# Recurrence of a hybrid decoder layer: sums of split tiles, key products in four array quarters, and the samples' chunk stacked on 128 partitions

## The chip, the cores and the metric

The kernel runs on one core of a Trainium2 chip. The metric is the device time of one execution in microseconds; of the kernel before, three runs were timed. The engines are named as in the profile: PE is TensorE (PEld its weight loads), DVE VectorE, ACT ScalarE, POOL GpSimd, SP SyncE, which issues most of the DMAs.

## What is computed

The reference is one step of a decoder layer with two branches, a recurrence and a sparse attention, between two feed-forward blocks. The change lies in the recurrence, for 512 tokens of one prompt and 4 new tokens of each of 8 sample sequences, with 8 heads of width 64. Cut to what matters:

```python
def rwkv7_time_mix(p, prev, s0, mu, w0, w2, a0, a2, g2, k_k, k_a, r_k, ln_w, ln_b):
    xs = p + (p_prev - p) * mu
    r, k, v, wd, ad, gd = jnp.split(xs, ...)
    log_w = -softplus(-(w0 + tanh(wd) @ w2)) - 0.5
    decay = exp(-exp(log_w))
    a = sigmoid(a0 + ad @ a2)                      # rate
    g = sigmoid(gd) @ g2                           # gate
    kk = heads(k * k_k)
    kk = kk * rsqrt(maximum(sum(kk * kk, -1), 1e-24))      # key norms
    k = k * (1 + (a - 1) * k_a)
    def step(S, inp):
        sa = einsum('bhij,bhj->bhi', S, -kk_t)
        S = S * w_t[:, :, None, :] + sa[..., None] * (kk_t * a_t)[:, :, None, :] + v_t[..., None] * k_t[:, :, None, :]
        return S, einsum('bhij,bhj->bhi', S, r_t)
    s_final, y = lax.scan(step, s0, (r_h, w_h, k_h, v_h, kk, a_h))
    y = group_norm(y) * ln_w + ln_b
    bonus = sum(r_h * k_h * r_k, -1) * v_h
    return (y + bonus) * g, p[:, -1], s_final
```

## The kernel before

Activations lie with features on the partitions and the 544 tokens (512 of the prompt, 32 of the samples) in the columns; matmuls over all tokens run in two halves of 272. Dense layers use split tiles: a tile is kept as a rounded half `hi` and a rest `lo`, both of type f32r, and a product is the sum of two or three f32r matmuls. The recurrence before the change uses plain f32 tiles throughout, except for the final output `yah`.

The recurrence handles the 8 heads in four pairs. I call a pair a head, as the code does (`rw_head`, `ht` = 0 to 3). Each head is a Python generator that goes through these pieces:

- `rw_front` (L1605): loads; decay rates; rate product with `a2t`; key norms, which are sums over 64 partitions by a matmul with the 0/1 matrix `blk` (`head_sums`, L1598, matmul L1602); decay sums, which are running sums over the 64 tokens of a chunk by matmuls with the 0/1 matrix `tri` (L1650); then elementwise work that gives the key tiles `ar`, `be`, `ka`.
- `rw_prompt` (L1689): the prompt in 8 chunks of 64 tokens. `products` (L1703, matmul L1710) multiplies keys by keys. A triangular system is then inverted in blocks of 16, 32 and 64: the blocks of 16 in fifteen small steps, whose row selections are matmuls (L1738: `sel` as the stationary tile, `dd` moving) and whose two small DVE operations a step are L173 and L179. Then come the inverse of 32 (from L1770 on), u1 and u2 (L1815), the chunk matrices (L1830), and seven steps from chunk to chunk (L1863).
- `rw_sample` (L1890): the same for the 8 short sequences as one chunk of 32 columns, with the matmuls of `by_head` (L1900), each with a `tile_position` in the array. After it the state is written out, and the bonus sums (a `head_sums` with a copy `brk` of `blk`, scaled by r_k) and the gate product with `g2t` (also L1602) follow.
- `rw_tail` (L1991): group norm and gate, output to `yah` (cast L2010, subtraction L179).

Four heads may be under way (`RW_LIVE`), and a head starts nine turns after the one ahead of it (`RW_LAG`); each turn of the loop advances every live head by one `yield`. That only sets program order and with it priorities. A scheduler of the tile framework sets each engine's queue from dependencies, free buffers and priorities, so that a small edit can move instructions of several heads against each other. Between the small products it also places a dense filler, `wob_steps` (L2031, matmul L288 in `dense_half`), at a lower priority. Tiles come from pools with a fixed number of buffers: a tile that has no free buffer waits until the readers of an older one are done. PSUM has two double-bank tiles `mm` and four single-bank tiles `sm`.

```python
        said = next(g_, heads)
        if said is heads:
            live.remove(g_)
        elif said is True:
            with tc.high_priority(offset=-WOB_OFF):
                next(wst, None)
```

## Time and profile before

| | |
|---|---|
| median of three runs | 1766.99 us (1765.64 to 1770.39) |
| profiled execution | 1762.41 us |
| its span | 1760.6 us |
| mean granted clock of TensorE in it | 0.979 of full speed |
| busy in the span | PE 1673.3 us (95%), DVE 876.6 (50%), ACT 612.8 (35%), POOL 245.9 (14%) |

The profile is one execution, recorded by the hardware. Busy time is the time in which an engine had an instruction running; matmuls overlap and their ends are modelled, so a busy PE need not be PE at its peak. PEclk is the share of full clock that TensorE was granted in a stretch (1.00 is 2.4 GHz, 0.50 is 1.2 GHz). The chain of work goes back from the last instruction: at each step to what released it, or to the instruction before it on its engine; its rows have a start, a length and a count of like instructions. Idle time stands with the engine and line that ended it. The recurrence lies between about 1000 and 1246 us of the span.

### The profile page before, as it was taken

The page shows a single profiled execution, that of the slowest core. Times are in us where ns is not written, and L with a number is a line of the kernel's source. Part 1 is how long each engine was busy: PE and PEld are TensorE (multiplying, and loading weights), DVE is VectorE, ACT ScalarE, POOL GpSimd, SP SyncE. Part 2 cuts the span into 40 slices and gives each one's busy share as a digit, 9 for nine tenths or more (in the row PEclk, how much of TensorE's full clock was granted, in tenths as well). Part 3 has the DMA queues.
Part 4 walks back from the last instruction along what each step waited for, and adds up shares of the span by engine and source line. Part 5 has one row for each costly group of instructions (what it writes and reads, how often), then busy time and mean ns, then how long its engine had stood idle before and what let it go on. Part 6 is the DMA issues. An engine that isn't in the chain of part 4 may idle for free.

```text
span 1760.6 us, 34894 instructions
## 1 busy us (share of the span) xinstructions
PE 1673.3 (95%) x14727; PEld 1518.0 (86%) x14727; DVE 876.6 (50%) x1835; ACT 612.8 (35%) x1121; POOL 245.9 (14%) x304
## 2 busy tenths in 40 slices
PE   5999999999999899899898999999899999999997
PEld 4888899999988798677786977777898999999996
DVE  6664323323325835555558376766767333333345
ACT  4343221221223543343445352332456321222223
POOL 6640000000000312535300011221011000000000
PEclk9999999999999999999999997999999999999998
DMA  7863553563434185565422331211651433223221
GB/s 269 307 198 114 179 192 109 173 204 118 146 110 101 49 280 170 156 211 164 141 74 85 117 94 45 72 28 35 208 139 45 125 87 94 85 83 98 83 74 52
DMA packets 261348, 225.01 MB, mean 128 GB/s; under 512 B 28948, under 2 KB 225983, under 8 KB 260936
## 3 DMA queue, kind: packets, MB, share of 16 engines
q1 hardware_dynamic: 244928, 180.39, 34.1%
q0 software_dynamic: 10368, 35.79, 6.2%
q10 hardware_dynamic: 5896, 6.60, 1.1%
q8 instruction: 116, 1.90, 0.4%
q14 instruction: 40, 0.33, 0.1%
HBM read 199.57 MB, written 23.17 MB: 127 GB/s over the span
## 4 chain that ended last, share of the span: by engine, by line
PE 78%; DVE 7%; issue 5%; ACT 3%; DMA 3%; POOL 3%; SPq 0%; POOLq 0%; ACTq 0%; DVEq 0%
PE mm L279 46%; PE mm L288 7%; PE mm L400 5%; PE sm L519 2%; PE sm L288 2%; POOL sraw L1300 1%; PE sm L1900 1%; PE mm L1602 1%; PE mm L2107 1%; PE sm L1246 1%; PE sm L1738 1%; DMA raw<-in_phi_w1t_dram 1%; DMA raw<-in_w_o_dram 1%; PE sm L1710 1%; PE mm L1208 1%
## 5 line engine op out<-in xcount | busy, mean ns | idle before, releaser
L261 ACT CAST whi<-raw 128x1024 fp32r<-128x1024 f32 (+2 forms) x178 | 177.3, 997 | 655.7 <-PE mm L279 594.8
L279 PE MATMUL mm<-uh,whi 128*128 128x272 f32 (+1 forms) x1888 | 397.5, 292 | 3.6 <-ACT qs L193 1.3
L279 PE MATMUL mm<-uh,wlo 128*128 128x272 f32 (+1 forms) x1888 | 392.9, 289 | 1.0 <-DVE wlo L179 1.0
L279 PE MATMUL mm<-ul,whi 128*128 128x272 f32 (+1 forms) x1888 | 392.3, 289 | 0.0
L179 DVE TENSOR_TENSOR wlo<-raw,whi 128x1024 fp32r<-128x1024 f32 (+2 forms) x178 | 206.1, 1158 | 263.0 <-ACT whi L261 261.6
L279 PEld LDWEIGHTS mm<-uh,whi 128*128 128x128 f32 x1888 | 298.4, 189 | 23.3 <-ACT hh L880 9.2
L279 PEld LDWEIGHTS mm<-ul,whi 128*128 128x128 f32 x1888 | 299.9, 189 | 1.0 <-issue 1.0
L279 PEld LDWEIGHTS mm<-uh,wlo 128*128 128x128 f32 x1888 | 297.6, 189 | 2.5 <-DVE wlo L179 1.4
L173 DVE TENSOR_TENSOR sg<-mm,sg 128x544 f32<-128x544 f32 (+1 forms) x47 | 32.3, 687 | 161.6 <-PE mm L279 159.1
L400 PE MATMUL mm<-cx,w1h 128*128 128x256 f32 x512 | 100.4, 291 | 3.7 <-ACT cx L352 1.9
L676 POOL TENSOR_TENSOR xT<-xT,mr 128x272 f32<-128x272 f32 x24 | 25.4, 1076 | 532.1 <-DVE xT L173 519.9
L279 PE MATMUL mm<-hh,wlo 128*128 128x256 f32 x480 | 99.5, 289 | 0.0
L279 PE MATMUL mm<-hh,whi 128*128 128x256 f32 x480 | 99.4, 288 | 0.0
L279 PE MATMUL mm<-hlo,whi 128*128 128x256 f32 x480 | 99.3, 288 | 0.0
L400 PEld LDWEIGHTS mm<-cx,w1h 128*128 128x128 f32 x512 | 82.6, 193 | 11.2 <-issue 6.7
L279 PEld LDWEIGHTS mm<-hh,whi 128*128 128x128 f32 x480 | 77.2, 188 | 1.7 <-ACT hh L880 1.7
L279 PEld LDWEIGHTS mm<-hh,wlo 128*128 128x128 f32 x480 | 77.2, 188 | 0.0
L279 PEld LDWEIGHTS mm<-hlo,whi 128*128 128x128 f32 x480 | 77.2, 188 | 0.0
L400 PE MATMUL mm<-cx,w1l 128*128 128x256 f32 x256 | 73.8, 288 | 0.0
L1300 POOL DMA_INDIRECT sraw<-in_cache_kv_sel_dram,idx x64 | 64.0, 1001 | 58.1 <-PE sm L1313 37.0
L821 DVE TENSOR_TENSOR rtmp<-mm,modT 128x32 f32<-128x32 f32 x32 | 6.1, 191 | 117.9 <-PE mm L279 117.9
L182 DVE SCALAR_TENSOR_TENSOR xT<-mm,modT,xT 128x512 f32<-128x512 f32 (+2 forms) x80 | 46.4, 582 | 35.5 <-PE mm L288 35.2
(566 smaller groups left out, 2978.3 us busy)
## 6 DMA issues: line engine op xcount, KB each, us to landing
araw<-in_w_ada_dram SPq DMA_DIRECT2D x56, 512.0 KB
raw<-in_ffn_w_gate_dram SPq DMA_DIRECT2D x44, 512.0 KB
raw<-in_ffn_w_up_dram SPq DMA_DIRECT2D x44, 512.0 KB
raw<-in_w_in_dram SPq DMA_DIRECT2D x36, 512.0 KB
raw<-in_ffn_w_down_dram SPq DMA_DIRECT2D x32, 448.0 KB
raw<-in_w_ada_dram SPq DMA_DIRECT2D x16, 512.0 KB
raw<-in_ffn_w_down_dram SPq DMA_DIRECT2D x16, 512.0 KB
sraw<-in_state_kv_win_dram SPq DMA_DIRECT2D x16, 256.0 KB
```

Source lines behind the costliest of these rows:

```text
L173: V.tensor_tensor(out, a, b, ALU.mult)
L179: V.tensor_tensor(out, a, b, ALU.subtract)
L182: V.scalar_tensor_tensor(out, a, s, b, o0, o1)
L261: S.copy(hv, raw)
L279: T.matmul(ps[:m, h, :n], ww[:, k, :m], xx[:, c0:c0 + n], start=(k == 0 and j == 0), stop=(k == nk - 1 and j == 2))
L288: T.matmul(ps[:, :n], ww[:, k, :], xx[:, c0:c0 + n], start=(k == 0 and j == 0), stop=(k == nk - 1 and j == 2))
L400: T.matmul(pss[:, o, 256 * v:256 * v + 256], ww[:, v, o, jj, :], xx, start=(jj == 0 and j == 0), stop=(jj == 7 and j == 2))
L519: T.matmul(hold["ps"][32 * q:32 * q + 32, :], silT[:, k, :], raws_[i][:, h * 512:(h + 1) * 512], start=(k == 0), stop=(k == KT - 1), tile_ ...
L676: G.tensor_tensor(n, n, mr, ALU.subtract)
L1208: T.matmul(ps[:, g, 0:nk], qT[64 * g:64 * g + 64, i, qt * 128:(qt + 1) * 128], kvt[br, 0][64 * g:64 * g + 64, 0:nk], start=True, stop=True)
L1246: T.matmul(acc[64 * g:64 * g + 64, kt * 128:], kvtok[br][:, kt, 128 + 64 * g:192 + 64 * g], pt_[g][:, 512 * kt:384 * kt + 512], start=(br ...
L1300: G.indirect_dma_start(out=t, out_offset=None, in_=seltab, in_offset=bass.IndirectOffsetOnAxis(ap=idx8[:, c * NB + b:c * NB + b + 1], axis=0))
```

## The change

Everything is in the recurrence; the arithmetic is the same up to rounding.

1. The 0/1 matrices `tri` and `blk` become f32r (a load into an ordinary tile and a cast on ACT). `tri4` gets a constant group of its own, "v".
2. Decay sums, key norms and bonus sums take their data as a split pair: a cast on ACT, a subtraction on DVE, then two f32r matmuls where one plain f32 matmul stood. The pairs come from tiles with the tag "er", of which there are two buffers. The bonus scales rk on ACT (r times r_k, then the product on POOL) instead of scaling `blk` on DVE.
3. The rate product has one half of the tokens in each row half of the array; for that `a2t` is loaded twice and part of `xwa` is copied by a DMA.
4. `products` interleaves both heads of a pair over four quarters of the array and two PSUM banks.
5. The selections take only the columns of `dd` that the step still needs.
6. The samples' chunk is stacked on 128 partitions: key pairs with be over ka, value pairs with the state's result over xv. The state's product becomes one of 64 rows where it was the sum of two of 32. Small DVE operations on two heads are issued one for each head (`each`), and one masked state tile is made on POOL instead of two.

```diff
+    for h in range(2):
+        SY.dma_start(a2t[64 * h:64 * h + 64, :], I["rw_a2"][0])
+    place_consts("r", rwp)
+    load_consts("v", rwp)
     tw = rwp.tile([65, TOK], F32, name="tw")
     G.memset(tw[64:65, :], 1.0)
     act(tw[0:64, :], xwa[0:64, :], AF.Tanh)
+    SY.dma_start(xwa[0:64, 272:], xdr[12][64:128, 272:])
...
+    cr = ee()[:, 0:384]
+    SY.dma_start(cr, I["consts"][:, CSPAN["r"][0]:CSPAN["r"][1]])
+    S.copy(cgrp["r"], cr)
+    def er():
+        return rt([128, TOK], "er", 2, F32R)
...
+    def head_sums2(src):
+        hi, lo = er(), er()
+        S.copy(hi, src)
+        sub(lo, src, hi.bitcast(F32))
+        ps = mm()
+        for h in range(2):
+            for x_ in (hi, lo):
+                T.matmul(ps[:, h, 0:272], C("blk"), x_[:, 272 * h:272 * h + 272], start=(x_ is hi), stop=(x_ is lo))
+        return ps
...
+        sgh, sgl = [er()[:, 0:NP].rearrange("p (t f) -> p t f", t=4) for _ in range(2)]
+        S.copy(sgh, sig[:, 0:4, :])
+        sub(sgl, sig[:, 0:4, :], sgh.bitcast(F32))
...
-            T.matmul(ps[:, h, 0:272], a2t[64:128, hs], xwa[64:128, 272 * h:272 * h + 272], start=True, stop=True)
+            R = slice(64 - 64 * h, 128 - 64 * h)
+            T.matmul(ps[:, h, 0:272], a2t[R, hs], xwa[R, 272 * h:272 * h + 272], start=True, stop=True)
...
-        ps = head_sums(C("blk"), sq)
+        ps = head_sums2(sq)
...
-                T.matmul(ps[:, t2 * 256:(t2 + 1) * 256], sig[:, 2 * tb + t2, :], C("tri"), start=True, stop=True)
+                for x_ in (sgh, sgl):
+                    T.matmul(ps[:, t2 * 256:(t2 + 1) * 256], x_[:, 2 * tb + t2, :], C("tri"), start=(x_ is sgh), stop=(x_ is sgl))
...
-        G.tensor_tensor(rk, xr, km, ALU.mult)
+        act(rk, xr, AF.Copy, scale=pcol(RK_ + ht))
+        G.tensor_tensor(rk, rk, km, ALU.mult)
...
         def products(lhs, o1_, o2_):
+            pss = [sm() for _ in range(2)]
+            for cp in range(4):
+                for c2 in range(2):
+                    c0 = cp * 128 + c2 * 64
+                    for h in range(2):
+                        H = slice(64 * h, 64 * h + 64)
+                        T.matmul(pss[h][64 * c2:64 * c2 + 64, cp * 128:(cp + 1) * 128], lhs[H, c0:c0 + 64],
+                                 ar[H, :, c0:c0 + 64], start=True, stop=True)
...
-                T.matmul(ps[:, k * 128:(k + 1) * 128], sel[:, 4 * k4 + k, :], dd.rearrange("p q t -> p (q t)"),
-                         start=True, stop=True)
+                n = 15 - 4 * k4 - k
+                T.matmul(ps[:, k * 128:k * 128 + 8 * n], sel[:, 4 * k4 + k, :], dd[:, :, 16 - n:], start=True, stop=True)
...
+        R = [[slice(64 * h + 32 * a, 64 * h + 32 * a + 32) for h in range(2)] for a in range(2)]
+        def each(f, out, *in_):
+            for h in range(2):
+                f(out[R[0][h]], *(x[R[0][h]] for x in in_))
...
-        by_head(lambda h: ps[HF[h], 0:32], lambda h: sas[HT_[h]], lambda h: gg[HT_[h], 1, :], 32, 64, stop=False)
-        by_head(lambda h: ps[HF[h], 0:32], lambda h: tk[HT_[h], 3, :], lambda h: gg[HT_[h], 3, :], 32, 64, start=False)
+        by_head(lambda h: ps[HF[h], 0:32], lambda h: tk[HF[h], 1, :], lambda h: gg[HF[h], 32:64])
...
-        for a, w_ in ((1, wsa), (2, wsv)):
-            by_head(lambda h: ps[HF[h], :], lambda h: tk[HT_[h], a, :],
-                    lambda h: w_[HT_[h]].rearrange("p b i -> p (b i)"), 32, 64, start=(a == 1), stop=(a == 2))
+        ws = rt([128, NB, 64], "wide")
+        G.tensor_tensor(ws, bc(tk[:, 1].unsqueeze(1), [128, NB, 64]), bc(bm.unsqueeze(2), [128, NB, 64]), ALU.mult)
+        ps = sm()
+        by_head(lambda h: ps[HF[h], :], lambda h: tk[HF[h], 0, :], lambda h: ws[HF[h]].rearrange("p b i -> p (b i)"))
...
-        brk = rt([128, 128], "brk")
-        ts(brk, C("blk"), pcol(RK_ + ht), None, ALU.mult, ALU.bypass)
-        ps = head_sums(brk, d["rk"])
+        ps = head_sums2(d["rk"])
```

The change also moves instructions, since the scheduler orders each queue anew. Numbers behind a name count tiles and differ between the two programs. The first place is on PE, the key norms of head 1. Before, they stand inside the sixteen-block inversion of head 0 (its selections are L1738):

```order
L1738 MATMUL sm_11070<-dd_11021,cst_t 128x128 x4
L1719 MATMUL sm_11083<-cst_g,ar_10954 128x128 x4
L1900 MATMUL sm_11089<-gg_11044 32x32 x2
L1900 MATMUL sm_11089<-tk_11035,gg_11044 32x64 x2
L1602 MATMUL mm_11194<-e_11172,cst_r 128x272
L1738 MATMUL sm_11096<-dd_11021,cst_t 128x128 x4
L1719 MATMUL sm_11109<-cst_g,e_10952 128x128 x4
L1900 MATMUL sm_11115<-ia_11046,abv_11094 32x32 x2
L1602 MATMUL mm_11194<-e_11172,cst_r 128x272
```

In the changed kernel they (L1623, mm_11235) stand behind that inversion and the decay sums (L1676), with the bonus sums of head 0 (mm_11486) and its gate product (L1612) behind them, ahead of the first step of the inverse of 32 (L1799):

```order
L1676 MATMUL sm_11285<-cst_r,er_11167 128x256
L1623 MATMUL mm_11235<-er_11231,cst_r 128x272
L1623 MATMUL mm_11235<-er_11232,cst_r 128x272
L1623 MATMUL mm_11235<-er_11231,cst_r 128x272
L1623 MATMUL mm_11235<-er_11232,cst_r 128x272
L1623 MATMUL mm_11486<-er_11482,cst_r 128x272
L1612 MATMUL mm_11548<-sgd,g2t 128x272 x2
L1623 MATMUL mm_11486<-er_11483,cst_r 128x272
L1623 MATMUL mm_11486<-er_11482,cst_r 128x272
L1623 MATMUL mm_11486<-er_11483,cst_r 128x272
L1681 MATMUL sm_11293<-cst_v,sig_11156 128x64
L1799 MATMUL sm_11299<-t_1533_11246,f_11015 32x32 x32
```

The norms moved from inside head 0's inversion to its end, and the bonus sums, which stood further down, moved up to them. Three split pairs (sig, the norms' er_11231 and er_11232, the bonus' er_11482 and er_11483) now follow one another through two buffers.

The second place is the same on DVE. Before, the norm chain of head 1 (the 544-column rows) stands between the inversion's small operations:

```order
L179 TENSOR_TENSOR x_1484_11023<-x_1484_11023,t_1485_11025 128x8x9
L185 TENSOR_SCALAR brk_12119<-cst_r,pv 128x128
L173 TENSOR_TENSOR t_1485_11025<-sm_11096,x_1484_11023 128x8x8
L182 SCALAR_TENSOR_TENSOR e_11199<-e_11120,pv,e_11198 128x544
L179 TENSOR_TENSOR x_1484_11023<-x_1484_11023,t_1485_11025 128x8x8
L173 TENSOR_TENSOR e_11197<-e_11197,e_11172 128x544
L173 TENSOR_TENSOR t_1485_11025<-sm_11139,x_1484_11023 128x8x7
L173 TENSOR_TENSOR wide_11189<-sm_11184,cst_t 128x512
L179 TENSOR_TENSOR x_1484_11023<-x_1484_11023,t_1485_11025 128x8x7
L1945 TENSOR_REDUCE sas_11191<-wide_11189 128x64
```

Now it comes behind the inversion's last step and the transpose L1783:

```order
L179 TENSOR_TENSOR x_1489_11044<-x_1489_11044,t_1490_11046 128x8
L173 TENSOR_TENSOR x_1532_11244<-x_1489_11044,cst_t 128x256
L1783 STREAM_TRANSPOSE t_1533_11246<-x_1532_11244 128x256
L1759 COPY x_1715_12283<-cst_t 128x128
L179 TENSOR_TENSOR er_11232<-e_11205,er_11231 128x544
L1666 TENSOR_SCALAR e_11228<-mm_11235 128x544
L179 TENSOR_TENSOR er_11483<-e_10980,er_11482 128x544
L182 SCALAR_TENSOR_TENSOR e_11230<-e_11148,pv,e_11229 128x544
L173 TENSOR_TENSOR e_11228<-e_11228,e_11205 128x544
L176 TENSOR_TENSOR e_11010<-e_11010,sm_11269 128x32
L185 TENSOR_SCALAR e_11228<-e_11228 128x544
L173 TENSOR_TENSOR e_11230<-e_11230,e_11228 128x544
```

The subtractions of the two new pairs (er_11232, er_11483) stand among the norm chain's rows.

The third place is on PE, the state product of the samples, whose rows are 512 columns wide. Before, a first wide row stands ahead of twelve dense matmuls (L288) and three behind them:

```order
L288 MATMUL sm_11311<-ybh_10556,whi_11307 128x272
L288 MATMUL sm_11311<-ybh_10555,wlo_11308 128x272
L1900 MATMUL sm_11295<-wide_11291,tk_11035 64x512
L1900 MATMUL sm_11295<-wide_11292,tk_11035 64x512 x2
L1778 MATMUL sm_11332<-x_1522_11204,w_1533_11256 32x32 x32
L1719 MATMUL sm_11375<-cst_g,e_10953 128x128 x4
```

Now one stands ahead of them (not among these rows) and one behind:

```order
L288 MATMUL sm_11349<-ybh_10555,whi_11345 128x272
L288 MATMUL sm_11349<-ybh_10556,whi_11345 128x272
L288 MATMUL sm_11349<-ybh_10555,wlo_11346 128x272
L1931 MATMUL sm_11335<-wide_11333,tk_11056 64x512
L1807 MATMUL sm_11370<-x_1532_11244,w_1543_11298 32x32 x32
L1748 MATMUL sm_11413<-cst_g,e_10973 128x128 x4
```

Four wide instructions became two; the dense rows and what follows kept their places.

## Rows read from the trace of the kernel before

**Rows 1.** The page: span, and busy time of each engine.

```profile
span 1760.6 us, 34894 instructions
...
PE 1673.3 (95%) x14727; PEld 1518.0 (86%) x14727; DVE 876.6 (50%) x1835; ACT 612.8 (35%) x1121; POOL 245.9 (14%) x304
```

**Rows 2.** Windows: stretch, length, then PE, PEld, DVE, ACT, POOL busy, PEclk, DMA share, GB/s.

```profile
1033.50:1055.60 22.10, 18.25 (x228) 14.27 (x228) 20.07 (x65) 11.13 (x24) 2.47 (x3) 0.99 0.41 113
1055.60:1079.80 24.20, 24.16 (x242) 18.32 (x244) 11.62 (x20) 3.31 (x6) 5.74 (x8) 0.59 0.18 47
1079.80:1107.50 27.70, 27.44 (x458) 21.66 (x458) 22.14 (x72) 11.36 (x23) 2.89 (x4) 1.00 0.13 31
1107.50:1127.30 19.80, 19.80 (x267) 15.14 (x266) 12.04 (x23) 6.67 (x16) 7.46 (x9) 0.91 0.26 70
```

**Rows 3.** Chain of work, passes of the full array: start us, us, what.

```profile
1001.36 6.26 PE mm L279 x48
...
1008.73 1.06 PE sm L1650 x4
...
1015.78 0.92 PE mm L1602 x4
...
1044.44 1.11 PE mm L1602 x4
...
1095.59 1.11 PE mm L1632 x4
```

**Rows 4.** Chain of work, products in two or four tiles of the array.

```profile
1033.57 1.59 PE sm L1710 x32
...
1046.68 1.04 PE sm L1940 x8
...
1088.20 1.03 PE mm L1830 x32
```

**Rows 5.** Chain of work, state products of heads 0 and 1, head 0's gate product.

```profile
1058.70 1.89 PE sm L1900 x2
...
1063.61 3.60 PE sm L1900 x6
...
1109.42 1.00 PE sm L1900 x2
...
1112.13 1.86 PE sm L1900 x6
...
1116.72 0.91 PE mm L1602 x2
...
1125.66 0.66 PE mm L1602 x2
```

**Rows 6.** Chain at 1078 and 1086 us, then timeline of PE at 640 us: short passes.

```profile
1078.11 0.64 PE sm L1683 x8
...
1086.38 1.09 PE sm L1738 x8
...
639.97 4.01 PE L1113 MATMUL sm<-x,raw 128*128 128x64 f32 x32
```

**Rows 7.** Lines by form, 1000 to 1246 us: busy us, mean ns | idle before, releaser.

```profile
L279 PE MATMUL mm<-uh,whi 128*128 128x288 f32 x32 | 9.4, 294 | 0.0
...
L2010 ACT CAST yah<-e 128x544 fp32r<-128x544 f32 x3 | 2.0, 669 | 2.9 <-DVE e L176 2.9
...
L179 DVE TENSOR_TENSOR yah<-e,yah 128x544 fp32r<-128x544 f32 x3 | 2.2, 720 | 0.0
...
L176 DVE TENSOR_TENSOR ia<-ia,sm 64x32 f32<-64x32 f32 x4 | 0.7, 172 | 0.4 <-PE sm L1900 0.4
```

**Rows 8.** Timeline of DVE inside head 0's inversion: start us, us, instruction.

```profile
1042.68 0.72 DVE L1641 TENSOR_SCALAR e<-mm 128x544 f32<-128x544 f32 x1 [0.30 <-PE mm L1602]
...
1045.93 0.78 DVE L182 SCALAR_TENSOR_TENSOR e<-e,pv,e 128x544 f32<-128x544 f32 x1
```

**Rows 9.** Waits of PE, 1000 to 1246 us: total us, times, longest us.

```profile
PE sm L1770 <- DVE t L1754: 2.3, 1, 2.3
```

More of the change, by code (lines that the diff above doesn't have):

```diff
@@ L203, in place_consts @@
         a, b = CSPAN[group]
-        cgrp[group] = p.tile([128, b - a], F32, name="cst_" + group)
+        cgrp[group] = p.tile([128, b - a], F32R if group == "r" else F32, name="cst_" + group)
     def load_consts(group, p):
@@ L1894, in rw_sample, with by_head @@
         HF = [slice(64 * h, 64 * h + 64) for h in range(2)]
-        HT_ = [slice(32 * h, 32 * h + 32) for h in range(2)]
-        def by_head(out, lhs, rhs, ko, mo, start=True, stop=True):
+        R = [[slice(64 * h + 32 * a, 64 * h + 32 * a + 32) for h in range(2)] for a in range(2)]
+        def by_head(out, lhs, rhs, start=True, stop=True):
             for h in range(2):
-                T.matmul(out(h), lhs(h), rhs(h), start=start, stop=stop, tile_position=(ko * h, mo * h))
-        ps = sm()
@@ L1911, in rw_sample @@
[L1911 to L1915 removed]
+                T.matmul(out(h), lhs(h), rhs(h), start=start, stop=stop,
+                         tile_position=(lhs(h).start_partition(), out(h).start_partition()))
+        def each(f, out, *in_):
+            for h in range(2):
+                f(out[R[0][h]], *(x[R[0][h]] for x in in_))
@@ new lines, in rw_sample @@
+        ps = sm()
+        for w, a, src in ((0, 0, be), (0, 1, ka), (1, 0, ar[:, 0, :]), (1, 1, xv)):
+            by_head(lambda h: ps[R[a][h], w * 64:(w + 1) * 64], lambda h: src[HF[h], NP:], lambda h: ident[HF[h], HF[h]])
+        tk = rt([128, 2, 64], "tk")
+        S.copy(tk, ps[:, 0:128].rearrange("p (w j) -> p w j", w=2))
+        ps = sm()
+        for a, src in ((0, be), (1, ka)):
+            by_head(lambda h: ps[R[a][h], 0:64], lambda h: src[HF[h], NP:], lambda h: ar[HF[h], :, NP:])
+            by_head(lambda h: ps[R[a][h], 64:96], lambda h: ar[HF[h], 0, NP:], lambda h: src[HF[h], NP:])
@@ L1922, in rw_sample @@
+        ps2 = sm()
+        by_head(lambda h: ps2[R[0][h], 0:64], lambda h: gg[R[1][h], 0:32], lambda h: tk[R[1][h], 1, :])
+        abv = rt([128, 96], "abv")
+        each(V.tensor_copy, abv[:, 0:32], ps[:, 0:32])
+        each(S.copy, abv[:, 32:96], ps2[:, 0:64])
         yield
         ps = sm()
-        by_head(lambda h: ps[HT_[h], 0:32], lambda h: abv[HT_[h], 0:32], lambda h: ia[HT_[h], :], 32, 32)
-        add(ia, ia, ps[:64, 0:32])
+        by_head(lambda h: ps[R[0][h], 0:32], lambda h: abv[R[0][h], 0:32], lambda h: ia[R[0][h], :])
@@ L1926, in rw_sample @@
+        each(add, ia, ia, ps[:, 0:32])
         yield
         ps = sm()
-        by_head(lambda h: ps[HF[h], 0:32], lambda h: tk[HT_[h], 0, :], lambda h: ia[HT_[h], :], 32, 64)
-        by_head(lambda h: ps[HT_[h], 64:128], lambda h: ia[HT_[h], :], lambda h: abv[HT_[h], 32:96], 32, 32)
+        by_head(lambda h: ps[HF[h], 0:32], lambda h: tk[R[0][h], 1, :], lambda h: ia[R[0][h], :])
+        by_head(lambda h: ps[R[0][h], 64:128], lambda h: ia[R[0][h], :], lambda h: abv[R[0][h], 32:96])
         u1T = rt([128, 32], "u1T")
@@ L1931, in rw_sample @@
         V.tensor_copy(u1T, ps[:, 0:32])
-        u2s = rt([64, 64], "u2s")
-        V.tensor_copy(u2s, ps[:64, 64:128])
+        u2s = rt([128, 64], "u2s")
+        each(V.tensor_copy, u2s, ps[:, 64:128])
         yield
@@ L1937, in rw_sample @@
         for w, lhs in enumerate((u1T, ar[:, 1, NP:])):
-            for h in range(2):
-                o = 64 * w + 32 * h
-                T.matmul(ps[o:o + 32, :], lhs[HF[h]], s0T[HF[h]].rearrange("p b i -> p (b i)"), start=True, stop=True,
-                         tile_position=(64 * h, o))
-        wide = rt([128, NB, 64], "wide", 2)
+            by_head(lambda h: ps[R[w][h], :], lambda h: lhs[HF[h]], lambda h: s0T[HF[h]].rearrange("p b i -> p (b i)"))
+        wide = rt([128, NB, 64], "wide")
         mul(wide, ps.rearrange("p (b i) -> p b i", b=NB), bc(bm.unsqueeze(2), [128, NB, 64]))
@@ L1945, in rw_sample @@
         V.tensor_reduce(sas, wide.rearrange("p b i -> p i b"), AX.X, ALU.add)
[L1946 removed]
+        each(lambda o, a, b: stt(o, a, -1.0, b, ALU.mult, ALU.subtract), tk[:, 1, :], sas, u2s)
         yield
         ps = sm()
[L1949 to L1950 removed]
+        by_head(lambda h: ps[HF[h], 0:32], lambda h: tk[HF[h], 1, :], lambda h: gg[HF[h], 32:64])
         ps2 = sm()
[L1952 to L1954 removed]
+        by_head(lambda h: ps2[HF[h], 0:32], lambda h: sas[R[1][h]], lambda h: C("i32")[R[1][h]])
         S.copy(y[:, NP:], ps[:, 0:32])
```

50 lines of the change are left out of this document (11 added, 39 removed).

## The prediction

> **What bounds the kernel now.** I read the page first, then the span by stretches, then the chain, then single instructions. The page gives a span of 1760.6 us in which TensorE is busy 95% [rows 1]; the profiled execution took 1762.41 us, 4.6 us (0.26%) under the median of the three runs, 1766.99 us. A busy PE says little, since ends of matmuls are modelled, so I took the part that the change touches, about 1000 to 1246 us, and cut it where the work changes. Stretch A of a head goes from its key products (L1710) to the first step of its 32-block inverse (L1770); stretch B goes from there to the next head's products. Rows 2 are A and B of heads 0 and 1. The reader should see two regimes. In B, PE is full and VectorE is about half busy (11.62 of 24.20 us, 12.04 of 19.80): work taken off PE shortens B. In A, VectorE is busy 20.07 of 22.10 and 22.14 of 27.70 us, because the sixteen-step inversion runs there, two small VectorE operations a step, each waiting for the last: work taken off PE mostly makes room. The longest wait of PE in the whole part, 2.3 us, is L1770's for a VectorE transpose at the end of A of head 0 [rows 9].
>
> The second thing to see is the clock. The granted clock is 0.59 of full speed in B of head 0, that is mostly the 1.2 GHz level, and 0.91 in B of head 1; elsewhere 0.99 or 1.00 [rows 2]. The 1.89 and 3.60 us of the state products of head 0 against 1.00 and 1.86 us for head 1 [rows 5] are the same instructions at the two levels.
>
> **What PE saves, part by part.** Plain f32 runs as two passes, split tiles as two f32r products, so the number of PE instructions stays and the price of one falls. 48 f32r passes of 256 and 288 columns take 6.26 us, 0.130 us each [rows 3]; I use that for each new pass.
> - Decay sums: L1650 x4 takes 1.06 us, two such groups a head [rows 3]. After: 8 x 0.130 = 1.04. Saves 1.08 a head.
> - Key norms: 0.92 us [rows 3] becomes 4 x 0.130 = 0.52. Saves 0.40.
> - Bonus sums: 1.11 us (head 0) [rows 3] becomes 0.52. Saves 0.59.
> - Rate product with a2t: 1.11 us for four passes [rows 3]. The two halves now sit in the two row halves of the array and end in different banks; L1940's eight passes of 512 columns, in four tiles, take 1.04 us [rows 4], so passes in different tiles run side by side. Two pass times instead of four: saves 0.55.
> - Key products: 32 passes in two tiles, 1.59 us [rows 4], become 32 passes in four tiles, which is the form of L1830: 1.03 us [rows 4]. Two products a head: saves 1.12.
> - State product of the samples: 1.00 + 1.86 us at full clock, 1.89 + 3.60 at half [rows 5]. Its eight passes become four, and the order puts the second half behind twelve dense matmuls, so the halves don't overlap: twice the first row, 2.00 (3.78 at half clock). Saves 0.86, for head 0 1.71.
> - Small sample products: four tiles in place of two, one product less; I estimate 0.3 a head from the products' ratio 1.03 : 1.59.
> - Narrower selections (L1738): eight passes of 128 columns take 1.09 us, 0.136 with the start, and 32 passes of 64 columns with a 128x128 stationary tile (L1113) take 4.01, 0.125 each [rows 6]. Half the columns cost the same, so I take nothing. The other bound is L1683, 0.64 us for eight passes of 64 columns with 128 weight columns from 64 rows, 0.080 each [rows 6]: by that 120 passes would save up to 120 x 0.045 = 5.4 us. L1113 is the nearer row (full height, plain f32).
>
> A rule stands beside this last choice. The Trainium skill (TensorE: Matmul & The Clock Gate, section "LDWEIGHTS (loading the stationary operand)") says that a weight load takes the time of its columns at 1.2 GHz, whatever its rows; 128 columns would be 107 ns by its formula. L1113 agrees with it, L1683 at 0.080 does not. By the rule the narrowing is worth nothing, by L1683's row up to 5.4 us.
>
> Sum on PE: 4 x (1.08 + 0.40 + 0.59 + 0.55 + 1.12 + 0.3) + 3 x 0.86 + 1.71 = 16.2 + 4.3 = 20.5 us.
>
> **What it adds.** A split costs a cast on ScalarE (0.669 us) and a subtraction on VectorE (0.720 us) [rows 7], three times a head: 2.0 us of ScalarE and 2.1 of VectorE. ScalarE also scales rk; it is busy 11.13 of 22.10 us at most [rows 2], and takes this beside other work. VectorE also gets four more small operations a head (the add to ia at 0.172 us [rows 7] is one of them; 0.7 us together) and loses the small brk product: some 2.5 us a head. GpSimd does one masked state tile where it did two, off the path. Two more loads and the xwa copy enter SP's queue ahead of the first head's own loads. The xwa copy waits for the tanh that reads xwa, and input-projection weights queue behind it; the trace of before has no row for that wait. I take nothing: those weights wait for a free buffer anyway, and the dense stretch before the recurrence uses them one by one. Were one late, it would cost at most one group of 48 passes, 6.26 us [rows 3].
>
> The new wait is the hand-over of the split tiles. "er" has two buffers, so one pair is alive at a time. The order shows what follows: in heads 1 to 3 the key norms now stand behind the decay sums, and the previous head's bonus sums behind them, almost back to back. Each pair can be written only when PE has read the last. For the norms PE waits for the end of its own last pass (0.29 us a pass from start to end [rows 7], though one starts every 0.13), cast and subtraction: 0.29 + 0.67 + 0.72 and the signals between them, which I put at 0.17 in all, about 1.85 us. For the bonus it waits for the cast alone, about 0.95, as the g2t product covers the subtraction. In heads 2 and 3 about 0.4 us of state products stand in between; head 0's norms have dense work beside them (1.0). Sum: 1.0 + (1.85 + 0.95) + 2 x (1.45 + 0.95) = 8.6 us of new PE waits, most of them at the end of A. Bounds: 4 us if the queues serve at once, 14 if VectorE and ScalarE have other work in front each time.
>
> **One gain is not in the edit's words.** In head 0's A the norm chain of head 1 stood inside the inversion: 0.72 and 0.78 us [rows 8], a product of the same 544 columns that I put at 0.72 too, and two more. It now comes after it, into B, where VectorE has room. That takes these 2.2 us and more off head 0's A on VectorE and pays for the additions there. In A of heads 1 and 2 most of it was behind the inversion already.
>
> **The sum by stretches**, against 1762.41 us:
> - before 1033.5: PE is dense; 1.08 + 0.40 + 0.55 - 1.0 = -1.0.
> - A of head 0: the samples' chain, which releases the decay sums on PE, loses three norm steps ahead of it (2.22 us) and gains 0.7: 1.5 us earlier. The decay sums save 1.08, norms and bonus 0.99, the hand-over adds 2.8: 0.8 us are left, and L1770's 2.3 us of waiting lies inside what the hand-over takes.
> - B of head 0: -1.7.
> - A of head 1: VectorE +1.4 on its chain, norms moved behind the inversion, hand-over 2.4, sums shorter: +0.7.
> - B of head 1: state product -0.86, and g2t, which stood here as 0.91 and 0.66 [rows 5], now fills a gap in A: -2.4.
> - A of head 2: +0.5. B of head 2: -1.3.
> - A of head 3, with no next front: +0.3. B of head 3 with the last bonus: -1.7. The tail: 0.
> Sum: -7.4 us. Of 20.5 us saved on PE, the waits take 8.6, and A, where VectorE sets the pace, most of the rest. That is 1755.0 us for an execution like the profiled one, or, from the median, 1766.99 - 7.4 = **1759.6 us**.
>
> **Rivals.**
> - *No measurable change.* Hand-over at its upper bound (14 us) and A wholly VectorE's: B keeps about 7 us, A and the front lose as much. For it: VectorE's 20.07 of 22.10 us in head 0's A. Or the four tiles don't overlap: 4.5 + 2.2 us of the saving fall away. Time 1763 to 1770; about 1766. Chance 0.25.
> - *Slower, by the clock.* Each A of heads 1 and 2 ends in more PE waiting than before, with small tiles next. Before, A of head 0 was the stretch with least PE work (18.25 of 22.10 us busy [rows 2]), and the clock fell behind it, to 0.59 for a stretch of 24.2 us; the granted clock of B of head 1 was 0.91. If B of heads 1 and 2 fall to 0.6 too, each doubles about 8 us more of half-speed time, costing some 8 us: 1759.6 + 16 = 1775.6. It decides where the granted clock of those two stretches falls below about 0.75: there the loss passes the gain. Against it: dense matmuls stand inside B and PE's work in A of head 1 is 27.44 of 27.70. Chance 0.17.
> - *More gain: PE sets A too.* Waits at their lower bound, A shortened by what PE saves, and head 0's clock recovering sooner: 20.5 - 4 = 16.5: 1750. With L1683's price for the selections 5.4 us more: 1745. For it: PE is counted busy nearly all of A of heads 1 and 2. Chance 0.18.
>
> **How the numbers follow.** A measurement of this kernel can tell about 0.3%, 5.3 us, from no change. The forecast, a gain of 5.3 to 13 us, has 0.40. Faster: 0.40 + 0.18 = 0.58; within: 0.25; slower: 0.17. The range runs from 1745, the third rival with the far price, to 1771, the first rival's upper end; it leaves out the deep end of the clock rival.
>
> **What would show it.** Right: sums at 0.13 us a pass; L1710's place at about 1.03 us for 32; state products at 2.0 us a head; gaps of 1 to 2 us on PE in front of the norm and bonus sums, released by ScalarE and VectorE; head 0's A shorter, A of heads 1 and 2 about as long. Wrong: A shrinking by 3 us or more a head (PE was the bound), gaps under 0.5 us, selections at 0.08 a pass, or a granted clock below 0.75 in B of heads 1 or 2.

## The result: slower by 0.6%, and the profile after

The changed kernel took 1774.03 us (median of 20 runs, 1769.38 to 1779.65), the kernel before 1761.63 us (20 runs, 1754.39 to 1770.39): a ratio of 1.0063 with a 95% interval of 1.0047 to 1.0080, 12.4 us by the medians. The forecast was 1759.6 us. The three runs of before that it started from lay 5 us above the median of the twenty; from 1761.63 it would have said 1754.2.

The page of the changed kernel, span and busy time (against [rows 1]):

```profile
span 1768.4 us, 34895 instructions
...
PE 1668.9 (94%) x14711; PEld 1517.1 (86%) x14711; DVE 882.6 (50%) x1859; ACT 624.6 (35%) x1146; POOL 241.3 (14%) x300
```

Busy times moved by a few us and do not explain it. The windows show where it lies: the same four stretches as [rows 2], A and B of heads 0 and 1 (stretch, length, busy PE, PEld, DVE, ACT, POOL, PEclk, DMA share, GB/s).

```profile
1030.59:1063.64 33.05, 27.43 (x228) 20.81 (x229) 22.43 (x68) 10.83 (x20) 3.06 (x4) 0.59 0.25 74
1063.64:1079.69 16.05, 16.04 (x237) 13.05 (x237) 11.84 (x22) 6.66 (x18) 6.84 (x8) 0.89 0.30 79
1079.69:1112.96 33.27, 29.15 (x465) 23.61 (x462) 23.07 (x78) 13.22 (x25) 1.79 (x3) 0.90 0.12 30
1112.96:1132.02 19.06, 19.05 (x257) 14.98 (x257) 11.72 (x23) 7.75 (x20) 7.98 (x9) 0.82 0.24 64
```

A of head 0 grew from 22.1 to 33.05 us, and its granted clock fell from 0.99 to 0.59: the half-speed time that stood in B before now begins in A. B of head 0 shrank by 8 us, mostly since its clock came back to 0.89. A of head 1 grew by 5.6 us at a clock of 0.90. By the same cuts the four A together went from 104.6 to 126.7 us, the first three B from 64.6 to 54.8. From the first decay sums to the end of the recurrence the half-speed time rose from 34 to 61 us.

The chain of work shows the prices and the half clock (start us, us, what):

```profile
1030.59 1.10 PE sm L1738 x32
...
1035.45 0.93 DVE dd L1757
1036.38 0.04 issue
1036.42 2.02 PE sm L1768 x8
...
1057.04 0.65 ACT er L1618
...
1057.72 0.74 DVE er L179
...
1058.50 0.84 PE mm L1623 x2
...
1065.55 1.00 PE sm L1931 x2
...
1088.36 1.06 PE sm L1768 x8
...
1142.38 1.03 PE sm L1768 x8
```

The key products cost 1.10 us for 32 passes (1.59 in [rows 4], 1.03 forecast). A group of eight selections takes 1.06 us at full clock (120 to 96 columns) and 1.03 (88 to 64 columns) against 1.09 for 128 columns in [rows 6], so narrowing was worth next to nothing, as taken. In head 0's A the same group takes 2.02 us: the clock had fallen when it began. The rule set beside that choice, the section "LDWEIGHTS (loading the stationary operand)" of the Trainium skill's page TensorE: Matmul & The Clock Gate, agrees with this trace: with half to seven tenths of the moving columns and the same 128 stationary ones, a pass still takes 0.13 us. L1683's row in [rows 6], 0.080 us a pass, remains against it.

The waits of PE in the recurrence (total us, times, longest) have the hand-over in them, against one long wait in [rows 9]:

```profile
PE sm L1681 <- ACT e L1987: 2.8, 2, 1.8
PE mm L1623 <- ACT er L1618: 2.7, 4, 0.9
PE sm L1892 <- DVE f L182: 1.9, 5, 0.6
PE sm L1799 <- DVE t L1783: 1.5, 1, 1.5
PE sm L1768 <- DVE dd L1757: 1.3, 1, 1.3
```

### The profile page after: what moved, and what is told of

The parts are those of the page before. It is cut to its first block, busy times and chain, and to the rows that moved or that the text cites. A ratio compares the mean times of both kernels' runs of the same rounds, so it can differ in the third digit from the quotient of the medians.

```text
span 1768.4 us, 34895 instructions
## 1 busy us (share of the span) xinstructions
PE 1668.9 (94%) x14711; PEld 1517.1 (86%) x14711; DVE 882.6 (50%) x1859; ACT 624.6 (35%) x1146; POOL 241.3 (14%) x300
## 4 chain that ended last, share of the span: by engine, by line
PE 78%; DVE 7%; issue 5%; ACT 4%; DMA 3%; POOL 3%; SPq 0%; ACTq 0%; POOLq 0%; DVEq 0%
PE mm L279 46%; PE mm L288 7%; PE mm L400 5%; PE sm L519 2%; PE sm L288 2%; PE sm L1931 1%; POOL sraw L1300 1%; PE mm L2133 1%; PE sm L1768 1%; PE sm L1246 1%; DMA raw<-in_phi_w1t_dram 1%; DMA raw<-in_w_o_dram 1%; PE mm L1612 1%; PE mm L1208 1%; DMA raw<-in_ffn_w_down_dram 1%
```

## A line that separates clock from work

Every run comes with its mean granted clock. The runs of the kernel before lie on a line: 1752.45 us at 0.986, 1760.17 at 0.981, 1768.25 at 0.976, 1771.53 at 0.974. Over 141 runs of it, taken beside all the experiments (1764.3 us and 0.9789 on average), least squares give 1.59 us per 0.001 of clock (correlation -0.96, 1.5 us of scatter around the line, 1770.4 us at 0.975). One kernel's spread of 25 us thus goes almost wholly with the clock. For another kernel two numbers follow: its mean clock, and how far its runs lie from that line, which is what its work and waits are worth at equal clock (the mean is good to about 1 us; the before-runs of one set lie 0.6 us under the line, those of another 1.0 over it). The line rests on clocks of 0.973 to 0.988 and is carried on below them; within the kernels of the table the slope is 1.3 us on average, so the distance of one with a clock far below, as no_stack17's, is rough. The changed kernel lies 2.1 us **under** the line, at a clock of 0.9713; the clocks of its own before-runs are not recorded, but their time, 1761.63, is the line at 0.9805. So, by this estimate, 0.0092 x 1587 = 14.6 us were lost by the clock and 2.1 gained.

| kernel | median us | ratio to before (95%) | mean clock | from the line, us |
|---|---|---|---|---|
| changed | 1774.0 | 1.0063 (1.0047 to 1.0080) | 0.9713 | -2.1 |
| er_pool | 1766.5 | 1.0030 (1.0007 to 1.0052) | 0.9724 | -6.7 |
| no_split | 1763.6 | 0.9993 (0.9971 to 1.0014) | 0.9782 | -3.4 |
| no_quarters | 1770.8 | 1.0057 (1.0032 to 1.0083) | 0.9736 | -0.7 |
| no_stack17 | 1786.6 | 1.0137 (1.0102 to 1.0171) | 0.9647 | -1.1 |
| late_split | 1772.2 | 1.0057 (1.0031 to 1.0082) | 0.9696 | -6.4 |
| no_split_no_q | 1767.1 | 1.0019 (0.9991 to 1.0047) | 0.9773 | -0.6 |
| stall_before | 1764.5 | 1.0020 (0.9992 to 1.0048) | 0.9786 | +0.1 |
| load_before | 1769.8 | 1.0010 (0.9992 to 1.0029) | 0.9777 | +3.0 |
| double_er | 1781.7 | 1.0079 (1.0058 to 1.0100) | 0.9718 | +6.3 |
| norms_er | 1776.6 | 1.0050 (1.0032 to 1.0067) | 0.9712 | -0.3 |
| decay_er | 1774.8 | 1.0035 (1.0022 to 1.0047) | 0.9716 | -0.8 |
| warm0 | 1775.1 | 1.0045 (1.0020 to 1.0070) | 0.9754 | +4.1 |
| warm0_er | 1769.1 | 1.0017 (0.9992 to 1.0041) | 0.9765 | +1.2 |
| fill_a_er | 1775.8 | 1.0064 (1.0040 to 1.0088) | 0.9693 | -3.9 |
| fill_a_before | 1773.6 | 1.0050 (1.0030 to 1.0071) | 0.9758 | +4.4 |
| fill0_er | 1776.9 | 1.0084 (1.0055 to 1.0112) | 0.9708 | -1.8 |
| fill4_er | 1775.1 | 1.0076 (1.0048 to 1.0104) | 0.9718 | -0.4 |
| fill0_nosplit | 1757.2 | 0.9959 (0.9934 to 0.9984) | 0.9815 | -4.4 |

## Experiments: one part undone

**er_pool**: the split pairs come from the pool of 544-column tiles.

```diff
-    NE, NF = 18, 14
+    NE, NF = 20, 14
-        return rt([128, TOK], "er", 2, F32R)
+        return rt([128, TOK], "e", NE, F32R)
```

> The changed kernel with the split pairs taken from the pool of 544-column tiles (20 buffers instead of 18 and 2 apart), so that a pair need not wait for the last one. Theory H (the hand-over of two buffers lengthens A): the norms go back inside the inversion of the head before, A of heads 1 and 3 loses most of its 5.5 and 4.3 us, the time falls from about 1774 to about 1764, level with before. Theory Q (the key products in four quarters starve PE and VectorE at the start of A, and the clock falls there): A of head 0 stays at 33 us with the granted clock near 0.6 from its start, the time stays above 1770. Theory V (the split costs VectorE and ScalarE work, wherever it stands): same or slower, 1774 to 1778.

Measured 1766.5 us: 4.6 us further under the line than the changed kernel (-6.7 against -2.1), at nearly the same clock (0.9724 against 0.9713). That is theory H's part: the two buffers cost 4.6 us. In its profile L1623 keeps two waits on PE, 1.4 us in all where the changed kernel has 3.9:

```profile
PE mm L1623 <- ACT e L1618: 0.9, 1, 0.9
...
PE mm L1623 <- DVE e L179: 0.5, 1, 0.5
```

A of head 0 stays long and at a low clock, as Q had it, so H is not the whole:

```profile
1030.40:1058.40 28.00, 22.74 (x221) 17.57 (x222) 20.79 (x67) 11.49 (x23) 3.04 (x4) 0.65 0.29 86
```

**no_split**: sums of unsplit tiles again (the hunks at L1650, L1602 and `brk` undone); all else as changed.

> The changed kernel with decay sums, key norms and bonus sums again as plain f32 products of unsplit tiles (brk and the product on GpSimd as before); quarters, narrow selections, stacking and the rate product in two row halves stay. Theories H and V: the time falls to before's 1762 or below, down to 1755 since the rest saves PE time. Theory Q: it stays at 1770 or more, with PE idle about 4 us ahead of the first selection of head 0 and the clock falling there. Theory H against V is told by er_pool.

1763.6 us, clock 0.9782, 3.4 us under the line. This is 10.5 us faster than the changed kernel: the splits together bring most of the lost clock. A and B of head 0 in its profile:

```profile
1028.80:1054.50 25.70, 19.14 (x229) 14.42 (x230) 23.31 (x70) 11.62 (x26) 4.25 (x3) 0.91 0.38 108
1054.50:1073.00 18.50, 18.50 (x239) 14.62 (x242) 8.46 (x18) 3.12 (x6) 3.25 (x6) 0.75 0.19 46
```

Together 44.2 us, against 49.1 in the changed kernel. The profiled execution was the fastest of the twelve (1751.8 us at 0.984), so the medians and mean clocks carry the comparison, and this profile overstates it.

**no_quarters**: `products` as before.

> The changed kernel with the key products one head of the pair after the other, each in one PSUM bank and two tiles, as before; all else as changed. Theory Q: the first selection of head 0 comes 1.4 us earlier, the clock stays at 1.0 in A of head 0, A of head 0 falls from 33 to 25 us or less, the time to 1765 or below. Theories H and V: 1774 plus 2 to 4 us, since the products' passes cost more again.

1770.8 us: Q falls; A of head 0 is as long without the quarters (32.5 us at a clock of 0.58). At equal clock it loses 1.4 us (-0.7 against -2.1), and without the splits the quarters are worth 2.8 us (no_split against no_split_no_q). I had put down 4.5.

**no_stack17**: `rw_sample` as before, the pool cut from 18 to 17 tiles for room.

> The changed kernel with the samples' chunk unstacked as before; the pool of 544-column tiles is cut from 18 to 17 to make room. If the stacking saves what I put down for it, about 5 us over the heads, the time rises to about 1779, or lies 5 us further above before's line of time over clock. If it saves nothing or costs: 1772 to 1774 or less.

1786.6 us, but by the clock (0.9647); at equal clock only 1.0 us behind the changed kernel. The smaller pool is mixed into this. With 18 tiles the unstacked form (**no_stack**) has no room: 60 kb a partition are wanted, 58.03 are left. So the price of the stacking stays open.

**late_split**: the split of sig moved to the decay sums.

```diff
         ts(sig[:, 0:4, :], sig[:, 0:4, :], 0.5, 0.5)
-        sgh, sgl = [er()[:, 0:NP].rearrange("p (t f) -> p t f", t=4) for _ in range(2)]
-        S.copy(sgh, sig[:, 0:4, :])
-        sub(sgl, sig[:, 0:4, :], sgh.bitcast(F32))
...
         wm1, wc, wi = ee(), ee(), ee()
+        sgh, sgl = [er()[:, 0:NP].rearrange("p (t f) -> p t f", t=4) for _ in range(2)]
+        S.copy(sgh, sig[:, 0:4, :])
+        sub(sgl, sig[:, 0:4, :], sgh.bitcast(F32))
```

> The changed kernel with the split of sig (buffers, cast, subtraction) moved from the rate piece of the front down to the decay sums, so that the pair is claimed after the norms' pair and its 0.6 us subtraction no longer stands ahead of the masking of head 0's key products on VectorE. Theory C (the time follows the half-clock stretches, and head 0's stall of PE ahead of its first selection sets off the longest of them): the stall shrinks by 0.6 us, part of the runs keep full clock in A of head 0, the median comes to about 1766, and the runs lie on before's line of time over granted clock (1752.5 us at 0.986, 1771.5 at 0.974) or below it. Theory H (the hand-over): the norms go back inside the inversion, A of heads 1 and 3 shrinks by 2 to 5 us each, the time is 1766 too, but the clock stays at 0.971 and the runs lie some 6 us under that line. Theory V: no change, 1774.

This fits H: 4.3 us further under the line with two buffers only, by claiming them in the order of use, and in its profile A of head 1 takes 26.4 us and A of head 3 25.4, against 33.3 and 26.9. The time itself is only 1.8 us less, and in head 0's A PE still waits 4.9 us for the bonus' pair. The clock did not come back (0.9696), so the subtraction ahead of the masking was not, by itself, what sets it off.

**no_split_no_q**: the kernel before with the rate product, the narrow selections and the stacking alone.

> The kernel before with only the rate product in two row halves, the narrow selections and the stacked samples; neither splits nor quarters. Theory C: with the stall as in before the clock is 0.980 or better, and what these parts save on PE shows: 1755 to 1760. If the parts save nothing at equal clock: 1763, like the changed kernel without the splits.

1767.1 us, 0.6 us under the line: these three parts together save nothing that can be told from nothing. I had put down 7.7 us on PE for them (2.2 for the rate product, 4.3 and 1.2 for the stacking).

## Experiments: what lowers the clock

**stall_before**: a spare wait in the kernel before.

```diff
+                if ht == 0 and h == 0 and lhs is be:
+                    for i in range(3):
+                        V.tensor_copy(o1_.rearrange("p c h t -> p (c h t)"), ps)
                 mul(o1_[:, :, h, :], pvw[:, :, 0, :], bc(mA.unsqueeze(1), [128, 4, 64]))
```

> The kernel before with three spare VectorE copies of 512 columns, some 0.6 us each, put between head 0's first key product and its masking: about 1.9 us of VectorE work and of PE waiting ahead of the first selection of head 0, and nothing else. Theory C: the clock falls in A of head 0, the mean granted clock from 0.980 to about 0.973, and the time rises by far more than 1.9 us, to 1770 to 1776. Against it (the clock does not hang on this wait): 1764 to 1765 at 0.980.

The forecast of theory C missed, but the run does not test it: no wait of PE came about. The norm and bonus sums of plain f32 went into the place, and PE was busy from head 0's first key product to its first selection (start and length, PE busy, PEld, and so on):

```profile
1029.47:1040.12 10.65, 10.65 (x100) 9.03 (x101) 8.27 (x19) 2.23 (x4) 0.00 (x0) 0.52 0.82 205
```

The clock fell at 1029.8 us, before the first copy began (1031.3), and came back after 10 us, before the inversion. Mean clock 0.9786, +0.1 us from the line: nothing was lost that can be told.

**warm0**: spare PE work in head 0's A.

```diff
+        if ht == 0:
+            with tc.high_priority(offset=-WOB_OFF):
+                wps = sm()
+                for i in range(12):
+                    T.matmul(wps[:, 0:272], ybh[0][:, i % 4, 0:128], ybh[0][:, i % 4, 0:272], start=True, stop=True)
         yield
...
+            if ht == 0 and k4 < 3:
+                with tc.high_priority(offset=-WOB_OFF):
...
             yield
```

> The changed kernel with spare PE work in A of head 0 and nothing else: four blocks of twelve f32r passes of 272 columns on the filler's data, whose results nobody reads, one block among the first key products and one behind each of the first three groups of selections; 48 x 0.130 = 6.2 us of passes. Theory C (head 0's A loses by the clock, which falls when PE idles ahead of the first selection): the granted clock in A of head 0 stays near 1.0 or comes back sooner, A of head 0 falls from 33 to 24 to 27 us, the mean clock rises from 0.971 to 0.975 or more, and the time falls by 3 to 8 us although work was added. Without theory C: A gets longer, by up to 6 us: 1774 to 1780 at the same clock.

A of head 0 in its profile:

```profile
1030.20:1059.70 29.50, 24.78 (x276) 20.43 (x276) 22.70 (x68) 10.82 (x20) 3.16 (x4) 0.92 0.32 82
```

With 6.2 us of passes more, A got 3.5 us shorter, at a clock of 0.92 in place of 0.59 (A and B together 47.8 us in place of 49.1). Over the runs the mean clock rose by 0.0041 (6.5 us) and the distance from the line by 6.2 us, what was added: the time stayed. So C is shown as far as this: PE work among the products and selections of head 0 holds the clock up there, and what it gives is what spare work costs. **warm0_er** is the same on top of er_pool:

> The same spare passes in the version whose split pairs come from the pool of 544-column tiles (1766.4 us, mean clock 0.9724). Theory C: the clock rises to 0.976 or more and the time falls to 1760 to 1764. Without it: 1766 to 1772.

Clock up by 0.0041 again, 1769.1 us: no gain either.

**load_before** adds the splits' casts and subtractions to the kernel before, unused; **double_er** is er_pool with each pass of the sums issued twice (`for h in (0, 0, 1, 1)`, likewise `t2`).

> The kernel before with the casts on ScalarE and subtractions on VectorE of all three splits added, their results unused, the sums plain f32 as before. Theory V: the mean clock falls from 0.979 to about 0.973 and the time rises to 1770 to 1775. Theory P: the clock stays at 0.978 or above, the time rises by 0 to 4 us.

> The version with split pairs from the pool of 544-column tiles (mean clock 0.9724, 6 us under before's line of time over clock), each f32r pass of the decay, norm and bonus sums issued twice into the same place: PE has as many passes' time in the sums as before the change (16 x 0.13 for a head's decay sums), VectorE and ScalarE work as in the split. Theory P (the clock falls since PE has less to do in A): the mean clock comes back to 0.976 to 0.979, the time stays near 1766 since added work and clock balance. Theory V (the VectorE and ScalarE work starves PE): the clock stays at 0.972, the time rises by some 5 us to 1771 to 1774.

Both fall out against their theories. The added VectorE and ScalarE work costs 2 to 3 us (its before-runs lie 1.0 us over the line) and no clock (0.9777 against 0.9774 of its before-runs), so the mere work, V, is not it. The passes given back cost 13 us at equal clock, of which some 8 are their own time (64 x 0.13) and 5, in the profile, a wait of PE at the end of head 0's A (5.4 us against 0.3 in er_pool); the clock stays at 0.9718. So P is not it either, as far as passes behind most of the selections go, which is where they stand.

**norms_er** (tri plain, decay sums unsplit) and **decay_er** (norms and bonus unsplit), both on er_pool:

> As the pool version, with the decay sums plain f32 again and only norms and bonus split. If the decay sums' split (its subtraction stands ahead of the masking of head 0's products, and its passes end A) lowers the clock: 0.977 or more and about 1760. If the norms and the bonus do: 0.973, 1768.

> As the pool version, with only the decay sums split; norms and bonus plain f32 (the bonus with rk scaled on ScalarE). The counterpart: 0.973 and 1768 if the decay sums' split lowers the clock, 0.977 and about 1761 if the norms and the bonus do.

Each kind alone brings the low clock, 0.9712 and 0.9716, and neither keeps er_pool's 6.7 us: the effects don't add. Their profiles show one reason. The longest wait of PE, L1770's in [rows 9], is 6.4 us in norms_er and 8.6 in decay_er, where 544-column operations of head 1 stand on VectorE between the last steps of the inversion; in the changed kernel it is 1.5, in er_pool 0.3.

The versions also differ in the order of PE's queue. Here it is, in letters, from head 0's key products to its inverse of 32 (P products, S a selection, n norm or split bonus sum, b plain bonus sum, g gate product, D decay sum, a dot for the small ones):

```
before         P.PSSSS.nSSSS.nSSSS.bbSSSg.g.DDDD.
no_split       P.PnSSSS.nb.SSSS.bgSSSS.gSSS.DDDD.
no_split_no_q  P.PSSSS.n.n.SSSS.bbSSSS.ggSSS.DDDD.
stall_before   P.PnnbbSSSS.SSSS.ggSSSS.SSS.DDDD.
load_before    P.PSSSS.SSSS.nSSSS.nSSS.b.b.gg.DDDD.
changed        P.PSSSS.SSSS.SSSS.SSS.DDDDDDDDnnnnnggnnn.
no_quarters    P.PSSSS.SSSS.SSSS.SSS.DDDDDDDDnnnnnggnnn.
late_split     P.PSSSS.n.SSSS.nSSSSnn.SSS.DDDDDDDD.nggnnn
er_pool        P.PSSSS.SSSS.SSSS.nSSS.nnn.DDDDDDDD.
norms_er       P.PSSSS.n.SSSS.nSSSSnn.SSS.DDDD.
decay_er       P.PSSSS.SSSS.SSSS.nSSSnn.n.g.g.DDDDDDDD.
double_er      P.PSSSS.SSSS.SSSS.nSSSnnnnnnn.DDDDDDDDDDDDDDDD.
```

The first five, at 0.9773 to 0.9789, have the bonus and gate products of head 0 beside or just behind the selections, before head 1's decay sums; in all but load_before they stand among the selections. Six of the others, at 0.9736 or less, have norms or split bonus sums there, but no gate products, or nothing. The order alone is not the cause, though: decay_er, at 0.9716, has two norms and two unsplit bonus sums as its four n, and the gate products behind them, like load_before at 0.9777. What separates the twelve profiles is the time that PE stands idle from head 0's first key product to its first selection: 0.95 us or less in the first five, 1.49 (no_quarters) to 2.43 us (changed) in the other seven, and in each of the seven the clock falls within a microsecond of the first selection. PE's timeline ahead of that selection (idle time and its releaser in brackets), first in decay_er:

```profile
1037.04 1.09 PE L1738 MATMUL sm<-ar,e 64*64 64x128 f32 x26 [0.33 <-DVE bE L173]
1039.39 1.79 PE L1768 MATMUL sm<-dd,cst_t 128*128 128x120 f32 x8 [1.25 <-DVE dd L1757]
```

then in load_before:

```profile
1037.36 1.59 PE L1719 MATMUL sm<-ar,e 64*64 64x128 f32 x32
1039.39 1.13 PE L1747 MATMUL sm<-dd,cst_t 128*128 128x128 f32 x8 [0.44 <-issue]
```

and in no_split, where the norms' first passes stand in the pause and the selections run at full clock:

```profile
1032.59 0.72 PE L1604 MATMUL mm<-e,cst_r 128*128 128x272 f32 x2 [0.70 <-ACT e L193]
1033.16 1.13 PE L1744 MATMUL sm<-dd,cst_t 128*128 128x120 f32 x8
```

A wait there does not decide it alone. warm0 and fill0_er (below) keep 1.26 and 1.24 us of it right ahead of the first selection, some 1.5 in all, with twelve dense passes among the key products, and run the first selections at full clock; in stall_before and no_split_no_q the clock had fallen some us earlier and was back after 10 us. That the pause makes the clock, and that the splits act through it, is an inference from one profile of each version and from warm0. No run changed the pause alone, so why the splits lower the clock stays open.

## Experiments: useful work in the pause

**fill_a_er** and **fill_a_before** hand out the dense filler behind each group of selections (`yield True` in the loop over `k4`) and no longer in the inverse of 32.

> The version whose split pairs come from the pool of 544-column tiles, with the dense filler (twelve L288 passes a time, 1.6 us) handed out behind each group of selections in A, where PE waits for VectorE, and no longer in the inverse of 32 in B. Theory C: useful passes in A keep the clock up there, A grows by less than B shrinks, the time falls to 1750 to 1758. Against it: the passes stand ahead of the next selections in PE's queue and lengthen A by what B loses, 1766; or B loses its clock without the dense passes, 1770.

> The kernel before with the dense filler moved in the same way from B to A. Theory C: the clock of head 0's B, 0.59 in the profile of before, recovers if the passes bridge the wait at the end of A; 1752 to 1758. Against it: 1762 or more, since A of heads 1 to 3 was full on PE already.

Misses: 1775.8 and 1773.6 us. In fill_a_er's profile the four A together took 134 us where er_pool's took 109, the first three B 60 where they took 69: A grew by far more than B lost, and B, without dense passes, lost its clock (19 of 20 us of B of head 1 at half speed).

**fill0_er**, **fill0_nosplit** and **fill4_er** add one turn of the filler between the two key products, in head 0, in head 0 of no_split, and in all heads.

```diff
         tmp = rt([128, 8, 16], "t16", 2)
-        yield
+        yield ht == 0
```

> The version with split pairs from the pool of 544-column tiles (1766.4 us, clock 0.9724, 6 us under before's line of time over clock), with one more turn of the dense filler handed out between head 0's first and second key products: twelve L288 passes, 1.6 us that the program has to do anyway, in the pause of PE ahead of the first selection. Theory C in its narrow form (that pause sets off the low clock of head 0's A): the clock does not fall at the start of A of head 0, the mean clock rises to 0.976 to 0.979, the runs stay some 6 us under the line, the time falls to 1757 to 1762, below both kernels. Against it: the clock falls a few us later all the same, 0.972, 1766 or more.

> The same one turn of the filler in the changed kernel without the splits (1763.6 us, clock 0.978, 3 us under the line), where that pause was short already. Theory C: clock 0.978 to 0.981, time 1758 to 1763. Against it: unchanged, 1763 to 1765.

> As fill0_er, with the turn of the filler in A of all four heads. If the pauses at the start of A cost clock in heads 1 to 3 too: 0.979 or more and 1755 to 1760. If PE is full there (before's A of head 1 has 27.56 of 27.82 us busy): no better than fill0_er, or 1 to 3 us worse.

fill0_er is a miss: 1776.9 us. In its profile, an execution 8 us under the median, the clock fell at 1048 us instead of 1036 and stayed down for 31 us. The pause was not filled, 1.24 us of it are left, and a new wait came at the end of A, where PE stood idle for the VectorE transpose:

```profile
1061.97 3.03 PE L1799 MATMUL sm<-t,f 32*32 32x32 f32 x64 [7.05 <-DVE t L1783]
```

fill4_er is the same (1775.1 us). With the splits gone:

```profile
1032.10:1055.80 23.70, 18.96 (x240) 14.82 (x240) 20.71 (x69) 10.93 (x25) 1.59 (x2) 1.00 0.42 104
1055.80:1073.30 17.50, 17.49 (x239) 13.84 (x239) 12.03 (x21) 4.39 (x8) 6.24 (x9) 0.80 0.33 87
```

A of head 0 keeps a clock of 1.00, A and B together take 41.2 us against 46.3 before and 49.1 in the changed kernel, and the whole 1757.2 us: faster than before by 0.4% (0.2 to 0.7%). Whether the turn of filler adds to no_split is not shown: their ratios to before have intervals that overlap, and at equal clock they lie 1 us apart. It is the version to keep: quarters, narrow selections, stacking and the rate product, no splits, one turn of the filler in head 0's A.

## Why the prediction was wrong

- **Sign and cause.** The rival "slower, by the clock", at 0.17, gave 1775.6 us; 1774.0 came. That the two agree is luck, since its place was wrong: not B of heads 1 and 2 (0.82 and 0.83 in the profile, above the 0.75 that it wanted), but A of head 0 first, 27 us at half speed from 1036 us on.
- **The step that failed** is "A of head 0: ... 0.8 us are left", with its neighbour "One gain is not in the edit's words". Both priced what leaves the inversion at full clock and counted it as a gain on VectorE. The wait for VectorE's transpose at the end of A did fall, from 2.3 to 1.5 us; but A of head 0 took 11 us more, 27 of its 33 us at half speed (in er_pool, without the hand-over, it takes 28.0 at a clock of 0.65), and with the sums unsplit (no_split) the kernel runs at a mean clock of 0.9782 in place of 0.9713, 10.5 us faster. [Rows 2] had the warning: PE busy 18.25 of 22.10 us in that stretch and a clock that fell behind it. I read it for what comes after A and not for A itself, from which the change takes PE work.
- **The sum.** At equal clock the change is worth 2.1 us, not 7.4. The hand-over measured 4.6 us, where I had 8.6 of waits, partly inside others, and its gaps on PE were 0.9 us at most, not 1 to 2: that mechanism was right and its size too large. With the hand-over taken out (er_pool) the change is worth 6.7, where the forecast comes to up to 7.4 + 8.6 = 16.0: the savings were the larger error. Of 7.7 us put down for rate product and stacking, no_split_no_q shows 0.6.
- **Prices.** Right: selections unchanged at 0.13 us a pass, products 1.10 for 32 (1.03 forecast), state product 1.00 us a half at full clock, and the decay sums, seven passes in 1.08 us with the tail of the last (timeline of PE; start us, us, instruction):

```profile
1104.92 1.08 PE L1676 MATMUL sm<-cst_r,er 128*128 128x256 f32 x7
...
1148.81 0.73 PE L1657 MATMUL mm<-xwa,a2t 64*128 64x272 f32 x4
```

  The same view of the kernel before has for the rate product:

```profile
1095.52 1.18 PE L1632 MATMUL mm<-xwa,a2t 64*128 64x272 f32 x4
```

  From its first start to its last end it fell by 0.45 us; I had put down 0.55. Cheaper passes gave little at equal clock; that A had no use for the room they made is my reading, no run shows it by itself.
- **The base.** Three runs with a spread of 5 us, from a kernel whose 141 runs spread over 25, were no ground for a forecast of 7; with the clocks of more runs the clock would have had a larger share of the chances.

## What to carry to other kernels

What a change saves on PE can be lost again by the clock. Here the split sums lost some 10 us of it (no_split), in a stretch whose pace VectorE sets; work given back at the end of that stretch did not bring it back (double_er), spare passes among the small ones did, at their own price (warm0). So look at the granted clock in and behind such a stretch, and at where PE stands idle after the scheduler has reordered. Check also that an experiment made the wait that it was to make: stall_before did not. Before comparing versions whose difference is under 1%, set each run's time against its mean granted clock; the distance from the line tells work and waits, the clock tells the rest. A split sum comes later by a cast and a subtraction, and pairs in two buffers should be claimed in the order in which they are used (4.3 us here at equal clock).

## What was not expected of the hardware

One kernel's runs differ by up to 25 us, and that follows the mean granted clock, 1.59 us for each 0.001, from 0.973 to 0.988 for the same program. And the clock can fall without any idle time of PE: in the kernel before it fell at 1116.5 us, where PE had been busy without a gap for 10 us with small tiles of the inverse of 32, the samples and dense passes between them.
